# Gather row tables tied to block 124 of U, activation blocks written in halves and full rows, sort constants loaded first

## The chip, the cores and the metric

One core of a Trainium2 chip runs the whole program. The metric is the device time of one execution in microseconds (us); several executions are taken and their median is compared. The core has five engines that run their own instruction queues in order: TensorE (PE) for matmuls, VectorE (DVE), ScalarE (ACT) and GpSimd (POOL) for elementwise work, and SyncE (SP), which here issues nearly all plain DMAs. POOL also issues the indirect DMAs (gathers).

## The reference, cut to what matters

The program is a two-layer decoder trunk for 256 tokens of width 1024. Each layer has a mixer (three attention-like branches) and then the expert stage, which is the part that the change touches:

```python
def peer_ffn(z, wq, subkeys, u_tab, v_tab):        # z: 256 tokens x 1024
    ...
    expert = i1 * PEER_NKEYS + i2                  # 8 heads x 16 picks of 16384 experts, per token
    gate = jax.nn.softmax(score, axis=-1)
    h = jnp.einsum('thkd,td->thk', u_tab[expert], zb)
    act = gate * jax.nn.gelu(h, approximate=False)
    return jnp.einsum('thk,thkd->td', act, v_tab[expert])
```

The tables `u_tab` and `v_tab` have 16384 rows of 1024 float32 numbers per layer.

## The kernel before, in words

The kernel does not gather rows of `u_tab`. It multiplies all 16384 rows with the 256 tokens, in 128 blocks of 128 experts. This is called U. For block `b`, `expert_h` loads 512 KB (`raw<-ut`, by SP, three `raw` buffers), ACT and DVE split it into a high and a low float32r part (`hi`, `lo`, in `split`, line 307), and PE does 24 matmuls of 256 columns (lines 311 to 313). The result goes through Gelu into the activation block `b`: 128 experts on the partitions, 256 tokens as columns. Blocks 0 to 47 lie in the tile `HA`, blocks 48 to 127 in `HB` (SPLIT = 48).

Beside U runs a generator, `gate_map`, which builds the gate factors, four tokens at a time, and multiplies them into all 128 blocks; `self.tok` counts the tokens done. When it has done all 256 tokens, the generator goes on into `lists`, which sorts experts: of blocks 0 to 107 (NC = 108) each partition keeps a list that puts experts used by the first 128 tokens alone first, then those used by both halves, then those used by the second half alone. The sort (fourteen rounds of MAX8 and MATCH_REPLACE8 on DVE) ends in two small tables, `rows` and `vrows`: which row of the activations, and which row of `v`, is next on each partition. It reads constants `quad` and `low`, and keeps its last intermediate, `own`, in a buffer of the tag `oh` (two buffers).

While U runs, the activation blocks 0 to 107 are also written to a DRAM buffer `dA` (shown as `act` in the trace), because the gather reads from there. The function `keep(h, done)` writes them, by SP: four blocks at a time (CHUNK = 4), the half `h` of the tokens in each, so that a row in DRAM is written as two pieces of 512 bytes. Half 0 may be written when 128 tokens are done, half 1 when 256 are. `keep` is called once per block and per half.

After U comes V (`experts_out`): out = activations times `v`. Blocks 108 to 127 are done whole, with plain loads of `v` (`raw<-v`); the first four of them come first. Blocks 0 to 107 are replaced by sorted lists: of the 108 list positions only 98 are done (`FROM1`, `TO0`, `TO1`), and 41 of these for one half of the tokens only. Each position takes two indirect DMAs on POOL, 512 KB of `v` (`HA<-v,vrows`) and 128 KB of activations (`HA<-act,rows`), both into room in the old `HA` tile: seven buffers for `v`, ten for the activations, six positions fetched ahead (FETCH = 6). The gather of activations needs all writes of `dA` to have landed. ACT and DVE then split both (`third` or `hi`/`lo`, and `ah`/`al`), and PE does 12 matmuls of 512 columns for a position with both halves, six for one with one half. Halfway through V stands an `If` on a flag that the sort set; its body is for lists that do not fit, and is skipped here. U and V together take more than half of a layer's time.

The order of instructions on each engine is made by a planner of the framework when the program is built: it moves an instruction forward if its own estimate says that it could run. `self.order(a, b)` tells it that `b` comes after `a` on their engine.

Of the kernel before, what the change touches and what calls it, by code (L numbers as in the profile page):

```python
# [7 lines left out]
F32 = mybir.dt.float32  # L8
# [3 lines left out]
I32 = mybir.dt.int32  # L12
U32 = mybir.dt.uint32
AF = mybir.ActivationFunctionType
OP = mybir.AluOpType
# [3 lines left out]
P = 128  # L19
T = 256  # L20
# [3 lines left out]
NB = 128  # L24
# [7 lines left out]
SPLIT = 48  # L32
# [11 lines left out]
NC = NB - ND  # L44
FROM1, TO0, TO1 = 18, 75, 98
IF_AT, FETCH = 45, 6
CHUNK = 4
ORDER = "rsrrrsrrcsrcrrrnrccrcsrcrrscrncsrrrgnrrrnaagSaSaSSagSgSaggSnggggSagSSnSaagaaaSgSgmSSSamamaSSaagSggSgggggSSmgmmgmmmmmmmmmmmmmmmmmm"
PACE_R, PACE_G = 1.5, 2.25

# [168 lines left out]
class Kernel:  # L219
# [851 lines left out]
    def peer(self, l):  # L1071
        nc, I = self.nc, self.I
        act, dve, pe = nc.scalar, nc.vector, nc.tensor
        with ExitStack() as ctx:
            hp = ctx.enter_context(self.tc.tile_pool(name=f"peer{l}", bufs=1))
            HA = hp.tile([P, SPLIT, T], F32, name="HA")
            sl = hp.tile([P, T // 4, 2, 4], F16, name="sl")
            gp = hp.tile([P, T // 4, 2, 4], F16, name="gp")
            with self.tc.tile_pool(name=f"route{l}", bufs=1) as rp:
                self.z = self.norm_t(self.pvt[:, PV_LN2:PV_LN2 + 8])  # L1080
                if l + 1 < self.layers:
                    self.pvt = self.cp.tile([P, PV_END], F32, tag="pvt", name="pvt")
                    nc.sync.dma_start(self.pvt, I["pv"][l + 1])
                sub = rp.tile([P, 16, P], F32, name="sub")
                nc.sync.dma_start(sub, I["subk"][l])
                qT = rp.tile([P, 16, T], F32, name="qTp")
                self.qdone = 0
                self.deep, self.turn = True, 2
                run = Pace(self.route(rp, sub, qT, (sl, gp)), PACE_R)
                for j in range(16):  # L1090
                    act.copy(qT[:, j], self.proj(I["wq"][l, j], self.z, "sc" if j < 2 else "mm"))
                    self.qdone = j + 1
                    run(1)
                for b in range(SPLIT):
                    self.expert_h(l, b, HA[:, b], None)
                    run(1)
                run(None)
            hp = ctx.enter_context(self.tc.tile_pool(name=f"late{l}", bufs=1))
            HB = hp.tile([P, NB - SPLIT, T], F32, name="HB")
            blk = lambda b: HA[:, b] if b < SPLIT else HB[:, b - SPLIT]  # L1100
            dA = self.dram.tile([NC * P, T], F32, name=f"act{l}")
            self.l, self.hdone, self.tok = l, 0, 0
            kept = [0, 0]

            def keep(h, done):
                b = kept[h]
                n = min(CHUNK, (SPLIT if b < SPLIT else NC) - b)
                if b < NC and self.tok >= P * (h + 1) and b + n <= min(SPLIT + done, NC):
                    src = HA[:, b:b + n] if b < SPLIT else HB[:, b - SPLIT:b - SPLIT + n]
                    hs = slice(h * P, (h + 1) * P)  # L1110
                    nc.sync.dma_start(dA[b * P:(b + n) * P, hs].rearrange("(b p) t -> p b t", p=P), src[:, :, hs])
                    kept[h] += n

            run = Pace(self.gate_map(hp, (sl, gp), HA, HB), PACE_G)
            for b in range(SPLIT, NB):
                self.expert_h(l, b, blk(b), hp, self.tok)
                self.hdone += 1
                run(1)
                keep(0, self.hdone - 1)
                keep(1, self.hdone - 1)  # L1120
            run(None)
            for h in range(2):
                while kept[h] < NC:
                    keep(h, self.hdone)

            if l + 1 < self.layers:
                tiles = [hp.tile([P, D], F32R, tag="oh", name="ready", bufs=2) for _ in range(2)]
                self.ready([I["wa"][l + 1, 0]], tiles)
            if l + 1 == self.layers:
                lnf = hp.tile([P, D], F32, tag="oh", name="lnf", bufs=2)  # L1130
                src = I["lnf"]
                nc.sync.dma_start(lnf, bass.AP(tensor=src.tensor, offset=src.offset, ap=[[0, P], [1, D]]))
                act.mul(lnf, lnf, D ** 0.5)
            self.xnew = self.experts_out(l, hp, HA, blk, dA, l + 1 < self.layers)
            for t in range(2):
                if l + 1 < self.layers:
                    nc.sync.dma_start(self.xd[1][t], self.xnew[t])
            if l + 1 == self.layers:
                self.final(self.xnew, lnf)
# [114 lines left out]
    def expert_h(self, l, b, dst, pool, tok=0):  # L1254
        p = self.proj(self.I["ut"][l, b], self.z)
        if tok < T:
            self.nc.scalar.activation(dst[:, tok:], p[:, tok:], AF.Gelu)
        if tok:
            tmp = pool.tile([P, T], F32, tag="gel", name="gel", bufs=2)
            self.nc.scalar.activation(tmp[:, :tok], p[:, :tok], AF.Gelu)  # L1260
            (self.nc.gpsimd if tok < T else self.nc.vector).tensor_tensor(dst[:, :tok], dst[:, :tok], tmp[:, :tok],  # L1261
                                                                          op=OP.mult)

    def route(self, rp, sub, qT, slots):
        nc, cst = self.nc, self.cst
# [107 lines left out]
    def gate_map(self, hp, slots, HA, HB):  # L1373
        nc = self.nc
        act, dve, pe = nc.scalar, nc.vector, nc.tensor
        sl, gp = slots
        iota2 = hp.tile([P, P, 2], F16, name="iota2")
        oh = hp.tile([P, 4, P, 4], F16, tag="oh", name="iota", bufs=2)
        iota = oh.bitcast(F32).rearrange("p a b c -> p (a b c)")[:, :P]
# [2 lines left out]
        cnt = self.pt([P, 2, P], "tp")  # L1382
        for t0 in range(0, T, 4):
            ts = slice(t0, t0 + 4)
# [24 lines left out]
                act.activation(hb[:, n:], pv[:, SPLIT + n:], AF.Copy, scale=1 / GS)  # L1409
            self.tok = t0 + 4  # L1410
            yield 1.8
        yield from self.lists(hp, cnt)

    def lists(self, hp, cnt):
        nc = self.nc
        act, dve, pe = nc.scalar, nc.vector, nc.tensor
        quad = hp.tile([P, 7, P], F32, name="quad")
        nc.sync.dma_start(quad, self.I["quad"])
        low = hp.tile([P, NC], I32, name="low")
        nc.sync.dma_start(low, self.I["low"])  # L1420
        four = lambda n: hp.tile([P, 2, 4, P], F32, tag="oh", name=n, bufs=2)
        ms, cf = four("ms"), four("cf")
        s = ms[:, 1].rearrange("p a b -> p (a b)")[:, :4 * NC].rearrange("p (a b) -> p a b", a=4)
# [51 lines left out]
        n = -(-NC // 8)  # L1475
# [7 lines left out]
        dve.tensor_scalar(own, ri, P - 1, 7, op0=OP.bitwise_and, op1=OP.logical_shift_left)  # L1483
        dve.tensor_scalar(ri, ri, 3 * P, 2, op0=OP.bitwise_and, op1=OP.logical_shift_right)
        dve.tensor_tensor(own, own, ri, op=OP.bitwise_or)
        self.rows = hp.tile([P, NC], I32, name="rows")
        self.vrows = hp.tile([P, NC], I32, name="vrows")
        dve.tensor_tensor(self.rows, own, low, op=OP.bitwise_or)
        dve.tensor_single_scalar(self.vrows, self.rows, self.l * NB * P, op=OP.bitwise_or)  # L1489
        yield 1.0  # L1490

    def final(self, x, lnf):
        nc = self.nc
# [25 lines left out]
```

## Time and profile before

| | us |
|---|---|
| median of 3 executions (2301.1, 2311.25, 2317.24) | 2311.25 |
| the profiled execution, own time | 2301.95 |
| its span, from first to last instruction | 2300.2 |

The profile is one execution. Times in it count from the start of the span. Layer 0's U blocks after 48 and its V lie between 533 and 1141 us, layer 1's between 1672 and 2286. "Busy" leaves out register, branch and DMA-issuing instructions; matmul ends are modelled, so a count of matmuls per microsecond tells more of PE than its busy share. The granted clock (PEclk) is a share of TensorE's full speed. Where a row ends in brackets, the first number is the time for which the engine had been idle before, and behind the arrow stands what ended it.

### The profile page before, as it was taken

How to read it: one execution, taken by the hardware profiler on the slowest of the kernel's cores; microseconds unless marked ns; L12 is line 12 of the kernel's file. 1: busy time of each engine (PE TensorE's matmuls, PEld its weight loads, DVE VectorE, ACT ScalarE, POOL GpSimd, SP SyncE). 2: the span in 40 equal slices, each digit the busy share in tenths (PEclk: the TensorE clock that was granted, in tenths of full speed). 3: DMA queues.
4: the chain of work that ended last, by engine and by line, in shares of the span. 5: the costliest groups of instructions: out<-in, count | busy, mean ns of one | idle time of the engine just before them, and what ended most of it. 6: DMA issues, size and time to landing. Idle time of an engine off the chain costs nothing. (4 is left out here: it accounts for less than half of the span.)

```text
span 2300.2 us, 43942 instructions
## 1 busy us (share of the span) xinstructions
PE 2236.1 (97%) x16662; PEld 2011.9 (87%) x16662; DVE 1701.4 (74%) x3699; ACT 1146.9 (50%) x2207; POOL 585.4 (25%) x601
## 2 busy tenths in 40 slices
PE   8999999999999999999999999999999999999898
PEld 8888888999999898877798888899999998987686
DVE  6578656996889876766666785769958898666566
ACT  5454434454544345655555444445544443455564
POOL 0001021000112135767600010300001220377674
PEclk9999989999999999999999999999999999999999
DMA  5644226556466887878655432455564758878785
GB/s 188 203 130 120 87 75 217 160 173 196 147 187 188 258 270 254 271 247 259 224 172 190 143 107 70 123 198 167 169 195 142 214 166 274 279 249 267 246 263 164
DMA packets 190152, 439.95 MB, mean 191 GB/s; under 512 B 30134, under 2 KB 90984, under 8 KB 189672
## 3 DMA queue, kind: packets, MB, share of 16 engines
q1 hardware_dynamic: 152008, 308.01, 42.4%
q0 software_dynamic: 37632, 128.48, 17.4%
q8 instruction: 135, 2.21, 0.4%
q14 instruction: 89, 0.73, 0.1%
q10 hardware_dynamic: 288, 0.52, 0.1%
HBM read 403.62 MB, written 33.32 MB: 190 GB/s over the span
## 5 line engine op out<-in xcount | busy, mean ns | idle before, releaser
L311 PE MATMUL mm<-zh,hi 128*128 128x256 f32 x3056 | 891.2, 292 | 9.9 <-ACT hi L307 7.1
L313 PE MATMUL mm<-zh,lo 128*128 128x256 f32 x3056 | 875.3, 287 | 7.4 <-DVE lo L307 7.4
L312 PE MATMUL mm<-zl,hi 128*128 128x256 f32 x3056 | 871.2, 285 | 0.0
L307 DVE TENSOR_TENSOR lo<-raw,hi 128x1024 fp32r<-128x1024 f32 (+1 forms) x468 | 590.5, 1263 | 204.3 <-ACT hi L307 202.6
L307 ACT CAST hi<-raw 128x1024 fp32r<-128x1024 f32 (+1 forms) x468 | 488.5, 1046 | 482.2 <-PE mm L312 310.3
L311 PEld LDWEIGHTS mm<-zh,hi 128*128 128x128 f32 x3056 | 588.3, 193 | 28.5 <-ACT hi L307 9.6
L313 PEld LDWEIGHTS mm<-zh,lo 128*128 128x128 f32 x3056 | 588.1, 192 | 18.9 <-DVE lo L307 10.0
L312 PEld LDWEIGHTS mm<-zl,hi 128*128 128x128 f32 x3056 | 588.7, 193 | 3.8 <-issue 2.9
L271 POOL DMA_INDIRECT HA<-act,rows x196 | 216.8, 1106 | 189.5 <-DVE vrows L1489 59.6
L271 POOL DMA_INDIRECT HA<-v,vrows x196 | 212.7, 1085 | 109.0 <-DVE third L307 38.1
L307 DVE TENSOR_TENSOR lo<-HA,hi 128x1024 fp32r<-128x1024 f32 x132 | 161.6, 1224 | 51.2 <-ACT hi L307 48.7
L1261 POOL TENSOR_TENSOR HB<-HB,gel 128x8 f32<-128x8 f32 (+24 forms) x100 | 82.0, 820 | 385.0 <-ACT gel L1260 336.1
L307 ACT CAST hi<-HA 128x1024 fp32r<-128x1024 f32 x132 | 138.5, 1049 | 30.2 <-PE po L313 25.9
L307 ACT CAST ah<-HA 128x256 fp32r<-128x256 f32 x196 | 79.3, 405 | 117.4 <-PE po L312 115.2
L307 DVE TENSOR_TENSOR al<-HA,ah 128x256 fp32r<-128x256 f32 x196 | 82.9, 423 | 67.5 <-ACT ah L307 24.4
L1409 ACT ACTIVATE HB<-sc 128x300 f32<-128x300 f32 (+38 forms) x128 | 44.8, 352 | 156.2 <-DVE HB L1407 153.2
L307 DVE TENSOR_TENSOR third<-HA,third 128x1024 fp32r<-128x1024 f32 x64 | 78.3, 1223 | 48.7 <-ACT third L307 48.0
L311 PE MATMUL sc<-hi,ah 128*128 128x512 f32 x280 | 94.3, 400 | 16.4 <-ACT hi L307 10.6
L312 PE MATMUL sc<-lo,ah 128*128 128x512 f32 x280 | 100.4, 402 | 1.1 <-DVE lo L307 1.1
L307 ACT CAST third<-HA 128x1024 fp32r<-128x1024 f32 x64 | 67.3, 1051 | 59.4 <-DMA HA<-v,vrows 35.9
L313 PE MATMUL sc<-hi,al 128*128 128x512 f32 x280 | 96.1, 401 | 0.0
L1389 DVE TENSOR_TENSOR oh<-iota,sl 128x1024 f16<-128x1024 f16 x128 | 87.4, 684 | 9.5 <-POOL iota L1381 4.8
(479 smaller groups left out, 3818.8 us busy)
## 6 DMA issues: line engine op xcount, KB each, us to landing
raw<-ut SPq DMA_DIRECT2D x256, 512.0 KB, 3.8
raw<-wa SPq DMA_DIRECT2D x102, 512.0 KB, 3.5
raw<-v SPq DMA_DIRECT2D x40, 512.0 KB, 4.6
raw<-wq SPq DMA_DIRECT2D x32, 512.0 KB, 3.9
act<-HB SPq DMA_DIRECT2D x60, 256.0 KB, 5.2
raw<-wbr SPq DMA_DIRECT2D x24, 512.0 KB, 3.6
act<-HA SPq DMA_DIRECT2D x48, 256.0 KB, 5.1
raw<-cw SPq DMA_DIRECT2D x16, 512.0 KB, 4.4
```

The source lines that it names most:

```text
L271: self.nc.gpsimd.indirect_dma_start(out=dst, out_offset=None, in_=src, in_offset=bass.IndirectOffsetOnAxis(ap=row, axis=0))
L307: return self.nc.scalar.copy(hi, src), self.nc.vector.tensor_tensor(lo, src, hi.bitcast(F32), op=OP.subtract)
L311: return [mm(p, lhsT=l[0], rhs=r[0], start=first, stop=False), mm(p, lhsT=l[0], rhs=r[1], start=False, stop=False), mm(p, lhsT=l[1], rhs=r ...
L312: mm(p, lhsT=l[0], rhs=r[1], start=False, stop=False),
L313: mm(p, lhsT=l[1], rhs=r[0], start=False, stop=last)]
L1261: (self.nc.gpsimd if tok < T else self.nc.vector).tensor_tensor(dst[:, :tok], dst[:, :tok], tmp[:, :tok], op=OP.mult)
L1389: dve.tensor_tensor(oh.rearrange("p n a i j -> p (n a) i j"), iota2[:, None].to_broadcast(full), two(sl), op=OP.is_equal)
L1409: act.activation(hb[:, n:], pv[:, SPLIT + n:], AF.Copy, scale=1 / GS)
```

## The change

- The two instructions that make `rows` and `vrows` move out of `lists` into a function `tables`, which is called after the loop over U; its first instruction is ordered behind the DVE instruction that finishes block 124 (NB - START).
- `keep` writes blocks of `HB` three at a time, not four. Half 0 is written only as long as the gate map has not done all 256 tokens. After that, blocks whose half 0 is in DRAM get their half 1 as before; the others are written once, both halves, in rows of 1024 bytes.
- The loads of `quad` and `low` are issued ahead of `gate_map`'s own constant (`iota`), not at the start of `lists`.

```diff
-CHUNK = 4
+CHUNK, START = (4, 3), 4
...
             def keep(h, done):
                 b = kept[h]
-                n = min(CHUNK, (SPLIT if b < SPLIT else NC) - b)
-                if b < NC and self.tok >= P * (h + 1) and b + n <= min(SPLIT + done, NC):
-                    src = HA[:, b:b + n] if b < SPLIT else HB[:, b - SPLIT:b - SPLIT + n]
-                    hs = slice(h * P, (h + 1) * P)
-                    nc.sync.dma_start(dA[b * P:(b + n) * P, hs].rearrange("(b p) t -> p b t", p=P), src[:, :, hs])
-                    kept[h] += n
+                m = min(CHUNK[b >= SPLIT], (SPLIT if b < SPLIT else NC) - b)
+                if h and b < kept[0]:
+                    m = min(m, kept[0] - b)
+                if b < NC and self.tok >= P * (h + 1) and b + m <= min(SPLIT + done, NC) and (h or self.tok < T):
+                    src = HA[:, b:b + m] if b < SPLIT else HB[:, b - SPLIT:b - SPLIT + m]
+                    ts = slice(h * P if b < kept[0] else 0, h * P + P)
+                    nc.sync.dma_start(dA[b * P:(b + m) * P, ts].rearrange("(b p) t -> p b t", p=P), src[:, :, ts])
+                    kept[h] += m
...
             for b in range(SPLIT, NB):
-                self.expert_h(l, b, blk(b), hp, self.tok)
+                ins = self.expert_h(l, b, blk(b), hp, self.tok)
+                if b == NB - START:
+                    late = ins
                 self.hdone += 1
                 run(1)
                 keep(0, self.hdone - 1)
                 keep(1, self.hdone - 1)
             run(None)
-            for h in range(2):
-                while kept[h] < NC:
-                    keep(h, self.hdone)
+            while kept[1] < NC:
+                keep(1, self.hdone)
+            self.order(late, self.tables(hp))
...
     def gate_map(self, hp, slots, HA, HB):
...
+        quad = hp.tile([P, 7, P], F32, name="quad")
+        nc.sync.dma_start(quad, self.I["quad"])
+        low = hp.tile([P, NC], I32, name="low")
+        nc.sync.dma_start(low, self.I["low"])
+        self.low = low
...
     def lists(self, hp, cnt, quad):
...
-        quad = hp.tile([P, 7, P], F32, name="quad")
-        nc.sync.dma_start(quad, self.I["quad"])
-        low = hp.tile([P, NC], I32, name="low")
-        nc.sync.dma_start(low, self.I["low"])
...
         dve.tensor_tensor(own, own, ri, op=OP.bitwise_or)
+        self.own = own
+
+    def tables(self, hp):
+        dve = self.nc.vector
         self.rows = hp.tile([P, NC], I32, name="rows")
         self.vrows = hp.tile([P, NC], I32, name="vrows")
-        dve.tensor_tensor(self.rows, own, low, op=OP.bitwise_or)
+        first = dve.tensor_tensor(self.rows, self.own, self.low, op=OP.bitwise_or)
         dve.tensor_single_scalar(self.vrows, self.rows, self.l * NB * P, op=OP.bitwise_or)
-        yield 1.0
+        return first
```

`expert_h` now returns its last instruction, the multiplication of the block by its Gelu (line 1261).

## Rows read from the trace of the kernel before

**Rows 1.** The page's first lines: the span, and the busy time of each engine with its share and instructions.

```profile
span 2300.2 us, 43942 instructions
PE 2236.1 (97%) x16662; PEld 2011.9 (87%) x16662; DVE 1701.4 (74%) x3699; ACT 1146.9 (50%) x2207; POOL 585.4 (25%) x601
```

**Rows 2.** Busy time by stretch of layer 0 (start:end, length, then for PE, PEld, DVE, ACT and POOL the busy time and the number of instructions, then granted clock, DMA share, GB/s).

```profile
533.00:545.00 12.00, 12.00 (x108) 11.91 (x107) 7.42 (x9) 5.82 (x11) 0.50 (x2) 1.00 0.74 244
...
785.00:805.00 20.00, 15.38 (x109) 14.34 (x108) 15.25 (x35) 6.32 (x10) 0.00 (x0) 0.91 1.08 344
805.00:831.00 26.00, 25.63 (x191) 25.64 (x192) 24.07 (x48) 12.01 (x18) 0.00 (x0) 0.87 0.66 204
831.00:845.00 14.00, 14.00 (x119) 14.00 (x119) 7.98 (x12) 6.66 (x10) 10.81 (x10) 1.00 0.86 270
845.00:858.00 13.00, 13.00 (x111) 13.00 (x110) 5.95 (x9) 5.40 (x9) 8.72 (x8) 1.00 1.02 402
```

**Rows 3.** The same view of layer 1, the stretch in which its half-1 writes run.

```profile
1923.00:1943.00 20.00, 14.65 (x113) 13.55 (x111) 16.04 (x37) 6.32 (x10) 0.00 (x0) 0.96 1.10 345
```

**Rows 4.** The instructions of line 1111 (the writes of `keep`) on SP's queue, in layer 0 from 640 to 769 us: count, issue time in ns (min/median/max), first and last start.

```profile
L1111 SPq DMA_DIRECT2D act<-HA x12: 377/805/2575, 671.6 to 681.6; - x12
L1111 SPq DMA_DIRECT2D act<-HB x12: 377/455/1382, 684.3 to 760.2; - x12
```

**Rows 5.** The same, from 769 to 831 us.

```profile
L1111 SPq DMA_DIRECT2D act<-HB x18: 450/714/1747, 778.7 to 803.2; - x18
L1111 SPq DMA_DIRECT2D act<-HA x12: 377/606/1252, 769.5 to 781.8; - x12
```

**Rows 6.** The DMA view of 769 to 805 us: packets by size, and the main queue's packets, MB and share of the time of 16 engines.

```profile
DMA packets 15986, 11.55 MB, mean 321 GB/s; under 512 B 568, under 2 KB 14975, under 8 KB 15982
...
q1 hardware_dynamic: 15982, 11.50, 104.4%
```

**Rows 7.** The main queue in the DMA view of 545 to 580 us, where nearly all traffic is loads in rows of 4 KB.

```profile
q1 hardware_dynamic: 1693, 6.15, 56.3%
```

**Rows 8.** DVE in order of time, layer 0 (start, duration, line, operation): the multiplications that finish blocks 99, 109 and 124 (line 1261), and the instruction that makes `vrows`.

```profile
775.15 0.42 DVE L1261 TENSOR_TENSOR HB<-HB,gel 128x256 f32<-128x256 f32 x1
...
816.02 0.42 DVE L1261 TENSOR_TENSOR HB<-HB,gel 128x256 f32<-128x256 f32 x1
...
831.18 0.22 DVE L1489 TENSOR_SCALAR vrows<-rows 128x108 int32<-128x108 int32 x1
...
857.49 0.42 DVE L1261 TENSOR_TENSOR HB<-HB,gel 128x256 f32<-128x256 f32 x1 [0.72 <-ACT gel L1260]
```

**Rows 9.** DVE in order of time, layer 1: the end of MAX8's last round, `vrows`, and block 124.

```profile
1964.96 0.60 DVE L1478 MAX8 ms<-cf 128x8 f32<-128x432 f32 x1
...
1968.81 0.22 DVE L1489 TENSOR_SCALAR vrows<-rows 128x108 int32<-128x108 int32 x1
...
1994.61 0.42 DVE L1261 TENSOR_TENSOR HB<-HB,gel 128x256 f32<-128x256 f32 x1 [0.72 <-ACT gel L1260]
```

**Rows 10.** SP's queue in order of time, layer 1: the load of the last norm's weights, which takes over a buffer of the tag `oh`.

```profile
1965.64 0.33 SPq L1132 DMA_DIRECT2D lnf<-lnf  x1
```

**Rows 11.** POOL in order of time, layer 0: gathers number 1, 6 (the first of `v`), 17 and 18, the gather of `v` for the tenth and the 37th position, and the first gather of `v` behind the `If`.

```profile
831.45 1.18 POOL L271 DMA_INDIRECT HA<-act,rows  x1 [59.60 <-DVE vrows L1489]
...
838.59 1.32 POOL L271 DMA_INDIRECT HA<-v,vrows  x1 [0.30 <-issue]
...
854.89 0.96 POOL L271 DMA_INDIRECT HA<-act,rows  x1 [0.30 <-issue]
870.32 2.01 POOL L271 DMA_INDIRECT HA<-v,vrows  x1 [14.47 <-DVE third L307]
...
882.35 0.94 POOL L271 DMA_INDIRECT HA<-v,vrows  x1 [0.81 <-DVE lo L307]
...
957.18 1.25 POOL L271 DMA_INDIRECT HA<-v,vrows  x1 [0.30 <-issue]
...
996.34 0.94 POOL L271 DMA_INDIRECT HA<-v,vrows  x1 [8.78 <-DVE third L307]
```

**Rows 12.** Time to landing of the gathers of `v` (both layers, 196 of them).

```profile
DMA to landing us min/median/max: 4.2/5.0/11.0
```

**Rows 13.** ACT in order of time at the start of V, layer 0: the second whole block's load is split; then the first gathered rows of `v` (`third`), then both operands of the third whole block; and the activations of the fourth. Below them the splits of the `v` rows of the tenth and the 37th position.

```profile
866.28 1.05 ACT L307 CAST hi<-raw 128x1024 fp32r<-128x1024 f32 x1 [2.07 <-DMA raw<-v]
...
867.51 1.04 ACT L307 CAST third<-HA 128x1024 fp32r<-128x1024 f32 x1
868.44 0.41 ACT L307 CAST ah<-HB 128x256 fp32r<-128x256 f32 x1
868.75 1.06 ACT L307 CAST hi<-raw 128x1024 fp32r<-128x1024 f32 x1
871.07 0.41 ACT L307 CAST ah<-HB 128x256 fp32r<-128x256 f32 x1 [1.26 <-PE po L312]
...
897.90 1.05 ACT L307 CAST hi<-HA 128x1024 fp32r<-128x1024 f32 x1 [0.53 <-PE po L313]
...
967.90 1.05 ACT L307 CAST hi<-HA 128x1024 fp32r<-128x1024 f32 x1
```

**Rows 14.** PE in order of time: the first matmuls of the third whole block of V.

```profile
871.11 0.63 PE L311 MATMUL sc<-hi,ah 128*128 128x512 f32 x2
```

**Rows 15.** The loads of the gate map's and the sort's constants on SP's queue, both layers (count, issue time in ns, first and last start).

```profile
L1380 SPq DMA_DIRECT2D iota<-iota x2: 327/327/327, 533.2 to 1672.2; - x2
L1418 SPq DMA_DIRECT2D quad<-quad x2: 424/425/426, 533.6 to 1672.6; - x2
```

More of the change, by code (lines that the diff above doesn't have):

```diff
@@ L1260, in expert_h @@
             self.nc.scalar.activation(tmp[:, :tok], p[:, :tok], AF.Gelu)
-            (self.nc.gpsimd if tok < T else self.nc.vector).tensor_tensor(dst[:, :tok], dst[:, :tok], tmp[:, :tok],
-                                                                          op=OP.mult)
+            return (self.nc.gpsimd if tok < T else self.nc.vector).tensor_tensor(dst[:, :tok], dst[:, :tok], tmp[:, :tok],
+                                                                                 op=OP.mult)
     def route(self, rp, sub, qT, slots):
@@ L1411, in gate_map, with lists @@
             yield 1.8
-        yield from self.lists(hp, cnt)
-    def lists(self, hp, cnt):
+        yield from self.lists(hp, cnt, quad)
+    def lists(self, hp, cnt, quad):
         nc = self.nc
         act, dve, pe = nc.scalar, nc.vector, nc.tensor
-        quad = hp.tile([P, 7, P], F32, name="quad")
-        nc.sync.dma_start(quad, self.I["quad"])
-        low = hp.tile([P, NC], I32, name="low")
-        nc.sync.dma_start(low, self.I["low"])
         four = lambda n: hp.tile([P, 2, 4, P], F32, tag="oh", name=n, bufs=2)
```

## The prediction

> **What bounds the kernel now.** I read the page's first lines, then busy time by stretch around the end of U, then SP, DVE, POOL and ACT in order of time there. PE is busy for 97% of the span and DVE for 74% [rows 1], so only a stretch in which PE falls below its rate can give time back. PE's full rate in U is read where nothing holds it: 119 matmuls in 14 us and 111 in 13 us, 8.5 per us at a granted clock of 1.00 [rows 2]; a block of 24 matmuls then takes 2.82 us.
>
> Three places matter to this change. First the burst of writes after the gate map has ended: 30 chunks of 256 KB between 769 and 803 us in layer 0 [rows 5]. From 785 to 831 us PE does 109 + 191 = 300 matmuls where 46 x 8.5 = 391 fit, so 91 are missing: 10.7 us, part of it through the clock, which was granted at 0.91 and 0.87 there after PE had run dry [rows 2]. Block 109 is finished 40.9 us after block 99, where ten blocks take 28.2 us: 12.6 us by that reading [rows 8]. Layer 1 loses 57 of 170 matmuls, 6.7 us, in 20 us of the same stretch [rows 3]. So the burst costs some 10 us per layer. Second the end of U, from 831 to 858 us: 17 gathers are issued there and the DMA engines move up to 402 GB/s, yet PE keeps its full rate [rows 2, 11]. Third V, where POOL issues a gather every 1.3 to 1.6 us without rest from 882 us on, some 10 to 15 us ahead of the splits that need them [rows 11, 13].
>
> **The table held back.** `vrows` is made at 831.18 us in layer 0 and 1968.81 in layer 1; block 124 ends at 857.49 + 0.42 and 1994.61 + 0.42 [rows 8, 9]. With `rows` and `vrows` behind it, the first gather moves from 831.45 to about 858.5 us, 27 us later, and in layer 1 by 26 us. DVE does the same two instructions, under 0.5 us together. On U this brings nothing, since PE is full in the stretch that the gathers leave.
>
> What is late next is the first `v` row set. It is the sixth gather, 838.59 - 831.45 = 7.1 us behind the first [rows 11]: 858.5 + 7.1 = 865.6, and with the median landing of 5.0 us [rows 12] it is there at 870.6. Today ACT splits it at 867.51, in front of the operands of the third whole block (868.44 and 868.75), in one in-order queue [rows 13]. If ACT's order stays, that split ends at 870.6 + 1.04 = 871.6, the block's `ah` at 872.0, its `hi` at 873.0 and `lo`, on DVE 1.2 us behind, at 874.3; PE's first four matmuls on `hi` take 0.9 us of this. PE wants the block at 871.11 [rows 14]. Stall: 1.9 + 0.4 = 2.3 us per layer. Bounds: nothing, if the planner puts the gathered split behind the whole block's, since the first four whole blocks need no gather; with a landing of 11.0 us [rows 12], 8.3 us. I take 2.3, as the median landing is the nearest row.
>
> Behind it in POOL's queue stand all other gathers. The first 17 take 854.89 + 0.96 - 831.45 = 24.4 us, so the 18th goes at 882.9 where it went at 870.32 (it had waited 14.5 us for its buffer). By the tenth position's `v`, four gathers on, POOL is at 888.9 where it was at 882.35: 6.6 us late, since the idle time before it has been used up [rows 11]. That lag stays, as POOL has no rest until the `If`. Positions had a lead (gather to split) of 897.90 - 882.35 = 15.5 us, and 967.90 - 957.18 = 10.7 us at the tightest place [rows 11, 13]. Less 6.6, and with V itself 2.3 later, 11.2 and 6.4 us are left, more than the 5.0 us of a landing. I take nothing; the bound is 11.0 - 6.4 = 4.6 us per layer. At the `If` POOL waits for the other engines, 8.8 us [rows 11]: a lag of 6.6 us ends there, and the second half of V is as before.
>
> `own` keeps its `oh` buffer 27 us longer. In layer 1 the norm weights' load, with U loads behind it on SP, takes over such a buffer; it goes at 1965.64, when MAX8 has just let go of the other one, and before `rows` [rows 9, 10]. It doesn't wait for `own`: nothing.
>
> **The writes.** `keep` runs once per block. Before, 24 chunks leave ahead of the end of the gate map, 12 of `HA` and 12 of `HB` [rows 4]. The gate map does 2.25 / 1.8 = 1.25 steps of four tokens per block, so 128 tokens are done after 25 blocks of `HB`, all after 51; 26 calls for half 0 lie between (blocks 25 to 50), 12 go to `HA` and 14 to `HB`, now three blocks each: 42, so that 18 blocks (90 to 107) are left for full rows. The burst becomes 12 chunks of 256 KB, 14 of 192 and six of 384: 32 issues in place of 30, and 8,064 in place of 7,680 KB, as 14 chunks of 192 KB went ahead and not 12 of 256. Rows of 512 bytes fall from 15,360 to 11,520, and 2,304 rows of 1 KB come.
>
> The price of a row: loads of 4 KB took 0.563 x 35 us x 16 / 1693 = 186 ns each [rows 7]. The burst's 15,982 packets took 1.044 x 36 x 16 = 601 us; less 1,007 loads at 186 ns, 414 us remain for 14,975 short ones: 27.7 ns [rows 6]. What a row of 1 KB costs is not in the trace: 46.5 ns as a quarter of a 4 KB row, 55.4 as two short ones. The 3,840 short rows saved are worth 106 us of engine time, the new rows cost 107 to 128: on 16 engines the burst grows by 0 to 1.3 us. Two SP issues more (0.6 to 0.7 us each [rows 5]) lie beside transfers. I take 0.5 us per layer, nearer the 4 KB price, and hold that the burst stays as harmful as it is: it still starts all at once, when the gate map ends.
>
> The Trainium skill (Advanced Engine Details and Errata, Clock Domains) gives 42 to 43 ns for an unobstructed row of 1 KB. By that the burst would shrink by 0.5 us per layer and the sum be 2 us less; no run here shows such a row, and the trace's 512-byte row at 27.7 ns is no unobstructed one.
>
> **The constants.** `quad` is issued at 533.6 us already, 0.4 us behind `iota`: the planner had moved it up [rows 15]. Now it is ahead of `iota`, and the gate map may start some 2 us later, the landing of 448 KB. DVE is busy for only 7.4 of 12 us there and PE is full [rows 2]; the sort's end no longer sets the gathers' start. I take nothing; without that cover it is 2 us per layer.
>
> **Sum.** Two layers of 2.3 + 0 + 0.5 + 0 = 2.8 us: 5.6 us on 2301.95, 2307.6 us. The profiled execution is 9.3 us under the median of 2311.25, and the executions differ by 16 us among themselves, so I set the median at half that offset: 2307.6 + 4.7 = 2312 us.
>
> **The rivals.** (a) The burst is eased: full rows and fewer short packets let the U loads through. For it: the loss sits exactly where these writes run. Against it: more bytes, one more chunk kind, the same start. It decides where a 1 KB row costs clearly under 46 ns (106 us / 2,304), or where the new order on SP lets a load pass earlier. From here on the base is 2301.95 + 4.7 = 2306.6. Half the loss returned is 10 us in all: 2306.6 - 10 = 2297; all of it, 21 us: 2286.
> (b) The gathers' absence helps U's tail. The one wait for a load there is 2.1 us before the split at 866.28 [rows 13]; taken away in both layers and with no stall in V, -4 us: 2302. The Trainium skill (DMA: Bandwidth & Descriptors, Issuing engines are not separate DMA queues) states that transfers of all issuers share the same 16 engines; the trace agrees (402 GB/s with both), but PE shows no loss by it.
> (c) POOL becomes V's bound: the head start of 24 us was needed. Landings grow as six row sets of 512 KB now meet the whole blocks' loads, PE waits 4 to 8 us at the start of V and 2 to 4.6 before the `If`: 8 per layer gives 2306.6 + 16 = 2323, the ends of both terms with the writes at 1.3 us (8.3 + 4.6 + 1.3 = 14.2 per layer) 2335. It decides where a landing takes over 6.4 us. For it: the leads shrink all the way to the `If`.
> (d) Nothing shows: the planner reorders the splits, and everything else is hidden: 2307.
>
> **Chances.** Forecast 0.42, (c) 0.25, (b) and (d) together 0.20, (a) 0.13. About 1% is what a measurement of this kernel tells from no change: under 2288 or over 2334. Only the full version of (a) goes below: 0.04. Of (c) the upper part goes above: 0.10. Within 1%: 0.86. The range takes in the half version of (a) and most of (c), and the spread of the executions: 2297 to 2331, with 1 in 10 left out at either end. The forecast's own range, with the V stall at 0 to 5 and the write term at 0 to 1.3 per layer, is 2307 to 2319.
>
> **What would show it.** In the profile after: the first gather at 858 us or later; about 32 writes between the gate map's end and block 107, with 300 matmuls or fewer in the 46 us that are 785 to 831 now; `third` at the start of V ending ACT's wait on a gather of `v`; leads 4 to 7 us shorter up to the `If`, the same behind it; POOL's wait at the `If` shorter than 8.8 us. Wrong, if PE's matmuls in the burst rise by 30 or more (rival a), or if waits on `HA<-v,vrows` put gaps into PE before the `If` (rival c), or if POOL still starts before block 124.

## The result, and the profile after

| | before | after |
|---|---|---|
| median of six executions each, same chip (us) | 2307.98 | 2321.85 |
| lowest to highest (us) | 2301.1 to 2317.24 | 2320.29 to 2325.76 |
| ratio after / before, 95% interval | | 1.0051 [1.003, 1.0072] |
| the profiled execution, own time (us) | 2301.95 | 2325.76 |

The change costs half a per cent: 0.0051 x 2308 = 11.8 us by the ratio, 13.9 by the medians. The forecast was 2312, inside a range of 2297 to 2331. The two profiled executions lie 23.8 us apart, since that of before is among its fastest and that of after the slowest of its six; some 10 us between the two profiles can't be put down to the change. So stretches are compared below, not ends.

Busy time by stretch, layer 0 of the kernel after, in the columns of [rows 2]:

```profile
785.00:805.00 20.00, 15.91 (x129) 15.16 (x127) 15.91 (x39) 6.38 (x11) 0.00 (x0) 1.00 1.08 342
805.00:831.00 26.00, 24.79 (x183) 24.58 (x184) 22.77 (x42) 12.05 (x19) 0.00 (x0) 0.87 0.69 211
831.00:845.00 14.00, 14.00 (x119) 14.00 (x118) 7.41 (x11) 6.55 (x10) 0.00 (x0) 1.00 0.60 178
845.00:858.00 13.00, 13.00 (x111) 13.00 (x110) 6.78 (x9) 6.35 (x10) 0.00 (x0) 1.00 0.60 193
```

PE does 129 + 183 = 312 matmuls in the 46 us of the burst; before it did 300 [rows 2]. U's end is full in both, 119 and 111. POOL is now idle there, and the DMA engines move 178 to 193 GB/s where they moved up to 402.

The writes, in layer 1 of the kernel after (count, issue time in ns, first and last start), first ahead of the end of the gate map, then behind it:

```profile
L1113 SPq DMA_DIRECT2D act<-HB x14: 360/434/2561, 1834.8 to 1888.9; - x14
...
L1113 SPq DMA_DIRECT2D act<-HA x12: 377/683/1711, 1823.1 to 1833.2; - x12
```
```profile
L1113 SPq DMA_DIRECT2D act<-HB x20: 386/620/1332, 1932.5 to 1955.1; - x20
...
L1113 SPq DMA_DIRECT2D act<-HA x12: 378/613/1290, 1920.8 to 1931.9; - x12
```

That is 32 issues in the burst, 20 of them of `HB`. The DMA view of 769 to 805 us answers to [rows 6]:

```profile
DMA packets 15002, 11.77 MB, mean 327 GB/s; under 512 B 616, under 2 KB 14056, under 8 KB 14998
...
q1 hardware_dynamic: 14998, 11.73, 106.4%
```

What a full row of 1 KB takes is read where nearly nothing else moves, from 1949.4 to 1953.4 us, in layer 1:

```profile
DMA packets 1528, 1.55 MB, mean 387 GB/s; under 512 B 62, under 2 KB 1513, under 8 KB 1528
...
q1 hardware_dynamic: 1528, 1.55, 110.7%
```

The start of V is where the profiles part. DVE (the table), POOL (the first, third, tenth and eleventh gathers) and ACT, all in layer 0 of the kernel after, in order of time:

```profile
858.78 0.27 DVE L1497 TENSOR_TENSOR rows<-ms,low 128x108 int32<-128x108 int32 x1
859.09 1.22 DVE L307 TENSOR_TENSOR ready<-raw,ready 128x1024 fp32r<-128x1024 f32 x1
860.23 0.21 DVE L1498 TENSOR_SCALAR vrows<-rows 128x108 int32<-128x108 int32 x1
```
```profile
859.35 2.01 POOL L271 DMA_INDIRECT HA<-act,rows  x1 [88.93 <-DVE rows L1497]
...
863.04 0.95 POOL L271 DMA_INDIRECT HA<-act,rows  x1 [0.30 <-issue]
...
873.13 0.95 POOL L271 DMA_INDIRECT HA<-act,rows  x1 [0.30 <-issue]
874.38 0.94 POOL L271 DMA_INDIRECT HA<-v,vrows  x1 [0.30 <-issue]
```
```profile
872.19 0.41 ACT L307 CAST ah<-HA 128x256 fp32r<-128x256 f32 x1 [1.45 <-PE po L312]
879.68 1.04 ACT L307 CAST hi<-HA 128x1024 fp32r<-128x1024 f32 x1 [7.09 <-DMA HA<-v,vrows]
880.64 0.40 ACT L307 CAST ah<-HB 128x256 fp32r<-128x256 f32 x1
880.95 1.04 ACT L307 CAST hi<-raw 128x1024 fp32r<-128x1024 f32 x1
```

Ten gathers of activations now go ahead of the first `v`, where five did [rows 11]: it leaves 15.0 us after the first gather, not 7.1. ACT, in order, waits 7.09 us for its rows (874.38 to 879.68), with the next whole block's operands (880.64, 880.95) behind it. PE, in order of time, layer 0 and layer 1, stops for what ACT splits behind its wait:

```profile
874.79 0.40 PE L313 MATMUL po<-hi,al 128*128 128x512 f32 x1
880.78 1.22 PE L311 MATMUL sc<-hi,ah 128*128 128x512 f32 x2 [5.59 <-ACT hi L307]
...
2033.51 0.73 PE L311 MATMUL sc<-hi,ah 128*128 128x512 f32 x2 [3.90 <-ACT hi L307]
```

In layer 1 the order of the gathers is the old one, five and then `v`, and ACT waits at another split, `third`. `fetch` gives the buffer `third` to each third position (`n % 3 == 2`), so this split needs the third gather of `v`, the eighth in all. The first gather of `v`, issued at 2019.77 us, landed after 4.1 us; the third, issued at 2022.69, after 8.4. POOL, layer 1, then the view of the third gather alone (who waited for it, for how many us and how often, and its landing), then ACT:

```profile
2012.81 1.08 POOL L271 DMA_INDIRECT HA<-act,rows  x1 [89.64 <-DVE vrows L1498]
...
2019.77 0.94 POOL L271 DMA_INDIRECT HA<-v,vrows  x1 [0.30 <-issue]
...
2022.69 1.75 POOL L271 DMA_INDIRECT HA<-v,vrows  x1 [0.30 <-issue]
```
```profile
L271 POOL DMA_INDIRECT HA<-v,vrows x1: 1752/1752/1752, 2022.7 to 2022.7; - x1
...
  ACT third L307: 6.0, 1
...
DMA to landing us min/median/max: 8.4/8.4/8.4
```
```profile
2031.16 1.04 ACT L307 CAST third<-HA 128x1024 fp32r<-128x1024 f32 x1 [6.00 <-DMA HA<-v,vrows]
```

To compare all kernels I cut U's end and V's start by four marks: the start of DVE's multiplications that finish blocks 99, 109 and 127, and the start of the split of the seventh gathered row set of `v`. Microseconds between them, layer 0 / layer 1:

| | 99 to 109 (burst) | 109 to 127 (U's end) | 127 to seventh `v` (V's start) |
|---|---|---|---|
| before | 40.9 / 39.8 | 52.5 / 51.8 | 19.6 / 20.3 |
| after | 40.7 / 41.0 | 52.7 / 54.0 | 26.9 / 25.4 |

V's start is longer by 7.2 and 5.1 us, 12.4 together, the size of the measured loss. From there to the `If` 98.2 us pass in layer 0 in both (888.11 to 986.29, and 893.92 to 992.11), and 98.5 and 98.8 in layer 1. From the seventh split to the last one V takes 255.2 and 256.3 us before, 257.4 and 258.6 after.

### The profile page after: what moved, and what is told of

Same layout as the page of the kernel before. It is cut to its first block, busy times and chain, and to the rows that moved or that the text cites. A ratio compares the mean times of both kernels' runs of the same rounds, so it can differ in the third digit from the quotient of the medians.

```text
span 2324.0 us, 43975 instructions
## 1 busy us (share of the span) xinstructions
PE 2245.5 (97%) x16662; PEld 2017.0 (87%) x16662; DVE 1702.2 (73%) x3699; ACT 1145.4 (49%) x2207; POOL 584.6 (25%) x601
## 5 line engine op out<-in xcount | busy, mean ns | idle before, releaser
L271 POOL DMA_INDIRECT HA<-v,vrows x196 | 210.5, 1074 | 80.2 <-DVE al L307 36.8
L307 ACT CAST hi<-HA 128x1024 fp32r<-128x1024 f32 x132 | 138.6, 1050 | 38.8 <-PE po L313 26.9
L307 ACT CAST ah<-HA 128x256 fp32r<-128x256 f32 x196 | 79.3, 405 | 119.1 <-PE po L312 114.1
L307 ACT CAST third<-HA 128x1024 fp32r<-128x1024 f32 x64 | 67.3, 1051 | 68.8 <-DMA HA<-v,vrows 42.6
```

What stands on the lines that cost most here:

```text
L271: self.nc.gpsimd.indirect_dma_start(out=dst, out_offset=None, in_=src, in_offset=bass.IndirectOffsetOnAxis(ap=row, axis=0))
L307: return self.nc.scalar.copy(hi, src), self.nc.vector.tensor_tensor(lo, src, hi.bitcast(F32), op=OP.subtract)
```

## The experiments

They ran in three groups, each on a chip of its own. The kernel before takes 2378.1, 2358.5 and 2360.5 us there, 2 to 3% more than in the first result; I call the chip of the first result the first chip, and take it for a fourth, though its number is not on record. Landing times are not shown in the traces of the groups. Each ratio is against the kernel before on the chip of its own group.

### The parts alone (first group)

The table held back, with old writes and old constants (the load of `low` and `quad` stays in `lists`):

```diff
+                ins = self.expert_h(l, b, blk(b), hp, self.tok)
+                if b == NB - 4:
+                    late = ins
...
+            self.order(late, self.tables(hp))
```

> The kernel before with one part of the change: rows and vrows made behind block 124; writes and constants as before. Theory G (the first rows of v come late to the start of V, because the held table puts ten gathers of activations ahead of them on POOL): 1.004 to 1.006 of the kernel before, PE waiting 4 to 6 us for the split of the first v rows at the start of each V. Theory W (the writes in three-block chunks and full rows make the burst longer): 0.999 to 1.001. Theory C (the constants put ahead of iota delay the gate map): 0.999 to 1.001.

The new writes alone, with the old table:

```diff
-CHUNK = 4
+CHUNK = (4, 3)
...
-            for h in range(2):
-                while kept[h] < NC:
-                    keep(h, self.hdone)
+            while kept[1] < NC:
+                keep(1, self.hdone)
```
(and the new `keep`)

> The kernel before with the new keep alone (three-block chunks, full rows for late blocks). Theory G: 0.999 to 1.002, no wait of PE at the start of V; the burst's matmul loss within 2 us per layer of that before. Theory W: 1.004 to 1.006, with the loss in the burst 4 to 6 us per layer larger. Theory C: 0.999 to 1.001.

The kernel after with the first gathers on POOL put in pairs, `v` first:

```diff
+            pair = [self.gather(I["v"], ...), self.gather(dA, ...)]
+            if not rest and n < 10:
+                chain.extend(pair[n >= 7:])
+                self.order(*chain[-2 - (7 > n > 0):])
```

> The changed kernel with POOL's first gathers ordered in pairs, v ahead of activations for each position, so that the first v rows are asked for as POOL's first gather and not its eleventh. Theory G: the wait of 4 to 6 us at the start of V is gone, 1.000 to 1.002 of the kernel before. Theory L (the total of POOL's late start is what counts, whatever comes first): the same 17 gathers start at the same time, so PE waits as long before the If, 1.004 to 1.006. Theories W and C: 1.004 to 1.006, unchanged.

The kernel after with the table tied to block 116 instead of 124:

```diff
-CHUNK, START = (4, 3), 4
+CHUNK, START = (4, 3), 12
```

> The changed kernel with START = 12: the table is made behind block 116, eight blocks (23 us) sooner. Theory G and theory L: POOL starts 23 us sooner, the waits at the start of V go, 0.999 to 1.002 of the kernel before. Theories W and C: 1.004 to 1.006, since writes and constants are as in the changed kernel.

| | ratio [95%] | burst | U's end | V's start |
|---|---|---|---|---|
| table held alone | 0.9989 [0.9969, 1.0008] | 39.8 / 40.6 | 52.2 / 52.2 | 31.3 / 27.3 |
| writes alone | 0.9981 [0.9955, 1.0008] | 42.7 / 41.8 | 63.8 / 60.8 | 19.7 / 20.3 |
| after, `v` first | 1.002 [0.9998, 1.0042] | 41.4 / 40.7 | 52.1 / 52.7 | 21.7 / 28.7 |
| after, block 116 | 0.9964 [0.9942, 0.9986] | 42.3 / 41.4 | 54.6 / 53.1 | 26.1 / 22.3 |

Theory G alone (the held table only costs, at V's start) falls here: V's start is 7 to 12 us longer per layer than with the early table, as it should be, and yet the table held alone costs nothing in the whole. The other side is in U's end. Busy time by stretch, first of the kernel with the writes alone (gathers beside U), then of the table held alone:

```profile
831.00:845.00 14.00, 14.00 (x117) 13.83 (x115) 6.24 (x8) 4.83 (x8) 11.14 (x10) 1.00 0.87 288
845.00:858.00 13.00, 6.61 (x29) 5.82 (x29) 2.77 (x4) 3.62 (x6) 6.82 (x7) 0.61 0.83 314
```
```profile
831.00:845.00 14.00, 14.00 (x119) 14.00 (x118) 7.40 (x11) 6.54 (x10) 0.00 (x0) 1.00 0.63 183
845.00:858.00 13.00, 13.00 (x111) 13.00 (x109) 6.11 (x8) 5.88 (x9) 0.00 (x0) 1.00 0.61 192
```

With gathers beside it PE does 29 matmuls in 13 us, and the granted clock is 0.61; without them 111 at 1.00. What PE lacks is a load of U: ACT, in order of time, with the writes alone:

```profile
846.65 0.38 ACT L1261 ACTIVATE gel<-mm 128x256 f32<-128x256 f32 x1
855.71 1.04 ACT L307 CAST hi<-raw 128x1024 fp32r<-128x1024 f32 x1 [8.68 <-remote]
```

("remote" stands for a releaser that this trace does not resolve; the instruction needs only `raw`, so I read it as the landing of the load.) What the DMA engines did in that wait shows in busy time from 847 to 855 us, and in the two queues of the DMA view: q0, which carries POOL's gathers, and q1, the plain transfers of SP. First the kernel with the writes alone, then the kernel before on the first chip, which has issued about as many gathers by then:

```profile
847.00:855.00 8.00, 5.67 (x24) 4.91 (x24) 1.34 (x2) 0.03 (x1) 5.31 (x6) 0.56 1.02 399
...
q0 software_dynamic: 725, 2.53, 79.3%
q1 hardware_dynamic: 194, 0.67, 23.0%
```
```profile
847.00:855.00 8.00, 8.00 (x69) 8.00 (x68) 3.59 (x6) 2.63 (x5) 6.26 (x6) 1.00 1.02 411
...
q0 software_dynamic: 604, 2.16, 67.5%
q1 hardware_dynamic: 313, 1.13, 34.7%
```

The engines are full in both. Where PE starves, the gathers hold 79% of them and U's loads get 0.67 MB; where it doesn't, the loads get 1.13 MB. (The share of 0.83 above is lower because hardly anything moved from 855 to 858 us, where the share was 0.19.) On this chip the early gathers make U's loads late, which [rows 2] didn't show for the first chip. I called the theory of both sides T.

Theory W (the writes lengthen the burst) gets 0.9981, no loss.

### Two repeats, the kernel before against itself, and both remedies together (second group)

The kernel after again, the kernel before again, the table held alone again, and `v` first with block 116 (both edits above):

> The changed kernel once more, beside the kernel before, so that its time stands beside the other runs of this call. Theory G (late first v rows at the start of V, nothing gained in U's tail): 1.004 to 1.006. Theory T (two-sided: where gathers in U's tail make the U loads late, the held table gives back some 10 us per layer there, and takes about as much at the start of V): 1.003 to 1.007 if the kernel before runs at about 2308 us, 0.997 to 1.002 if it runs at about 2378 us as in the runs before this one.

> The kernel before itself, for its trace beside the others of this call. Theory T: if it runs at about 2378 us, PE loses 8 us or more between the end of the gate map's writes and block 124, where 17 gathers run beside the U loads, as it does in the kernel with the new writes alone; at about 2308 us it loses nothing there. Theory G: nothing lost there in either.

> The kernel before with the held table alone, once more. Theory T: within 0.2% of the changed kernel of this call (writes and constants do nothing). Theory W (the writes cost or give something): the changed kernel differs from it by 0.3% or more.

> The changed kernel with the table behind block 116 and POOL's first gathers in pairs, v first. Theory T: neither loss is there in full: 0.994 to 0.999 on a run like the slow ones, 0.999 to 1.002 on one like the first. Theory G: 0.999 to 1.001 on both.

| | ratio [95%] | burst | U's end | V's start |
|---|---|---|---|---|
| after | 1.0033 [1.0014, 1.0053] | 40.7 / 41.6 | 52.1 / 53.9 | 31.6 / 27.1 |
| before against itself | 1.0025 [1.0001, 1.005] | 39.8 / 39.0 | 54.8 / 64.8 | 19.7 / 20.3 |
| table held alone | 1.0024 [1.0003, 1.0045] | 41.2 / 42.6 | 52.7 / 52.2 | 26.9 / 27.2 |
| after, `v` first, block 116 | 1.0005 [0.9981, 1.0028] | 40.1 / 39.4 | 49.7 / 51.0 | 25.1 / 22.3 |

The kernel before against itself reads 1.0025: on these chips a difference under about 0.3% can't be told from none, and the 1.0024 and 1.0033 say hardly more than that. Its trace repeats the finding on U's end, now in the kernel before itself. Busy time by stretch, layer 1:

```profile
1980.00:2000.00 20.00, 18.77 (x153) 18.36 (x152) 11.49 (x22) 7.49 (x11) 9.52 (x10) 1.00 0.77 253
2000.00:2016.00 16.00, 9.18 (x38) 8.12 (x38) 4.49 (x6) 4.08 (x6) 7.84 (x8) 0.60 0.78 289
2016.00:2032.00 16.00, 16.00 (x132) 16.00 (x132) 7.05 (x10) 6.60 (x10) 0.00 (x0) 0.98 0.51 155
```

38 matmuls in 16 us while POOL issues eight gathers, 132 as soon as it issues none. From 2000 to 2008 us the gathers' queue held 93.5% of the DMA engines and the loads' 6.9%, with the old writes, so the new writes are not what starves PE. T had put this loss at 8 us or more at a time of about 2378 us; at 2366 layer 1 lost 13 against the first chip (64.8 for 51.8), layer 0 only 2 (54.8 for 52.5).

### Where the price of a late table shows clearly (third group)

The table tied to block 127 (START = 1); `v` first with START = 8; the kernel before with `v` first; the kernel after a third time:

```diff
-CHUNK, START = (4, 3), 4
+CHUNK, START = (4, 3), 1
```

> The changed kernel with START = 1: the table behind block 127, three blocks (8.5 us) later still. Theory T (the price is the wait for the first v rows at the start of V; U's tail has no more to give): the first six positions come 7 to 10 us later in each layer than in the changed kernel, so 14 to 20 us in all, 1.006 to 1.009 of it, and the stretch from block 109 to block 127 stays at 52 to 54 us. Theory L (POOL's lag, absorbed by leads of 10 us and more and ended at the If): within 0.2% of the changed kernel.

> The changed kernel with the table behind block 120 and POOL's first gathers in pairs, v first: the first v rows are asked for some 27 us sooner before they are needed than in the changed kernel (11.4 us by the table, 14 us by the order). Theory T: the start of V as in the kernel before (block 127 to the seventh position in 20 to 23 us, not 26 to 31), U's tail at 50 to 53 us; 0.994 to 0.997 of the changed kernel of this call, and 0.997 to 1.001 of the kernel before. Theory W or C: as the changed kernel.

> The kernel before with POOL's first gathers in pairs, v first; table, writes and constants as before. Theory T: the first rows are there long before V needs them in either order, so nothing changes at the start of V; 0.998 to 1.002. If the order on POOL by itself were worth something, 0.995 to 0.998.

> The changed kernel once more beside these three. Theory T: 1.003 to 1.006 of the kernel before on a run like the first, 0.998 to 1.004 on a slower one; block 127 to the seventh position takes 25 us or more in both layers.

| | ratio [95%] | burst | U's end | V's start |
|---|---|---|---|---|
| after, block 127 | 1.0113 [1.0082, 1.0145] | 40.8 / 38.6 | 52.7 / 54.4 | 39.5 / 36.3 |
| after, `v` first, block 120 | 1.0009 [0.9976, 1.0041] | 42.3 / 41.2 | 51.8 / 59.9 | 25.2 / 19.6 |
| before, `v` first | 0.9991 [0.9966, 1.0015] | 41.7 / 40.0 | 63.2 / 54.0 | 19.8 / 20.3 |
| after | 1.0019 [1.0, 1.0038] | 40.1 / 40.4 | 52.0 / 52.8 | 29.3 / 25.3 |

Three blocks later is the one clear difference: 1.0113. POOL (the first gather, and the eleventh, the first of `v`), ACT and PE at V's start, in order of time, of the kernel after with block 127:

```profile
868.18 2.22 POOL L271 DMA_INDIRECT HA<-act,rows  x1 [97.71 <-DVE rows L1497]
...
882.69 0.94 POOL L271 DMA_INDIRECT HA<-v,vrows  x1 [0.31 <-issue]
```
```profile
887.08 1.04 ACT L307 CAST hi<-HA 128x1024 fp32r<-128x1024 f32 x1 [10.97 <-DMA HA<-v,vrows]
```
```profile
888.17 1.22 PE L311 MATMUL sc<-hi,ah 128*128 128x512 f32 x2 [12.28 <-ACT hi L307]
```

It is the picture of the kernel after with the gathers 8.2 us later (they start at 860.02 us there, on the same chip); PE's stop grows from 5.6 to 12.3 us. Against the kernel after of its group the time is 2385.35 / 2363.91 = 1.009, the upper end of T's 1.006 to 1.009.

Taken together, on the three slower chips (each figure the mean of one profiled execution's two layers per kernel): with the early table (writes alone, before again, before with `v` first) U's end takes 60.2 us and V's start 20.0; with the table at block 124 and the planner's order of gathers (held alone twice, after twice) 52.5 and 28.2. Holding it back saves 7.7 us per layer and costs 8.2. That is +1.0 us for both layers; the four ratios are 0.9989, 1.0024, 1.0033 and 1.0019, with a mean of 1.0016, or 3.9 us, in the noise of 0.25% beside it. From the seventh split of `v` to the last one they take the same, 278.1 us per layer with the early table and 279.2 with the late one. At block 127 the sum of both stretches is 92.2 and 90.7 against 80.2: +22.5 us, and 0.0113 x 2360 = 26.7 was measured (the profiled execution, at 2372.49, is the fastest of its six, so the two needn't meet closely). So T holds for when the table is made, by the stretches and by the one ratio that stands out; its forecasts for the remedies do not, as the next paragraph says.

The remedies are not settled. The order of POOL decides V's start in layer 0: 21.7 us with `v` first at block 124 (table of the first group), against 26.9 to 31.6 in the four without. In layer 1, where only five gathers of activations go ahead anyway, the wait at `third` went from 5.6 to 6.5 us to 0.3, but V's start got no shorter (28.7 against 25.3 to 27.3): other waits took its place, some of which the trace doesn't resolve. Block 116 shortens V's start to 22.3 in layer 1. T's forecast for block 120 with `v` first failed: 0.994 to 0.997 of the kernel after of its group, where 2366.27 / 2363.91 = 1.001 came. There the gathers meet U's loads again. U's end takes 59.9 us in layer 1, and from 2036 to 2044 us PE does 27 matmuls, with 73.5% of the DMA engines for the gathers' queue and 21.1% for the loads'. For block 116 with `v` first T had 0.994 to 0.999, and 1.0005 came. 0.9964, 1.0005, 1.0009 for the versions with an earlier table don't agree, and the remainder of V differs by some 10 us from one profile to the next. No version beats the kernel before by more than the noise on two chips.

## Why the prediction came out as it did

The forecast was right in its range and its direction, and not in size: 5.6 us were added for the change, 11.8 to 13.9 came. The parts were not run alone on the first chip; what is said of it rests on the stretches of its two profiles.

**The step that was mis-sized** is the one at V's start: "What is late next is the first `v` row set. It is the sixth gather, 838.59 - 831.45 = 7.1 us behind the first". The kind of loss was right: a wait on `HA<-v,vrows` in ACT's queue, with the third whole block's operands behind it, and a gap in PE. The term was put at 2.3 us per layer; V's start grew by 7.2 and 5.1. Two inputs were wrong before any run:

- The split at 867.51 [rows 13] is of `third`, so it is not of the first row set of `v` but of the third. That is the eighth gather, issued at 841.47 us, 10.0 us behind the first.
- The landing was the median of all 196 gathers, 5.0 us. The first seven of `v`, the ones in question, took longer already then. Their landing in layer 0, before:

```profile
DMA to landing us min/median/max: 6.6/8.5/9.9
```

In layer 1 both show. ACT waited for the third row set, which left 9.9 us behind the first gather and took 8.4 us to land: 18.3 us, where the prediction had 12.1. With 10.0 in place of 7.1 and the landing left at 5.0, its own sum gives 5.2 us. In layer 0 the orders on POOL and ACT changed as well. ACT took the first row set first, and that was now the eleventh gather, 15.0 us behind the first, with a landing of 5.2 us. The order of the gathers had been read off the old trace, where the table was ready long before. Ten gathers of activations go ahead where another DVE instruction stands between `rows` and `vrows` (here `ready`, so that `vrows` starts 1.45 us behind `rows`). So it is in layer 0 of all five profiles with the table at block 124 and the planner's order on POOL; at block 127 ten and eight go ahead, with such an instruction in both layers; and wherever none stands between, in that order, five do. That the planner orders them so because of this split fits every layer, but is argued: no run moved only that split. That the order is what costs in layer 0 is shown by the run with `v` first (V's start 21.7 instead of 26.9 to 31.6).

PE also ran slower after the stop of 5.59 us: the granted clock was 0.50 from 880.7 to 884.3 us, the lower of its two levels, with eight matmuls in 3.6 us, and 1.00 behind it, with 17 in 3.7. This was not in the sum either; it is in the 7.2.

**POOL's lag, taken as nothing**, held up to the `If`. From the seventh `v` to there 98.2 us pass in both kernels. The lead of the 37th position, which the prediction took for the tightest place, shrank to 7.7 us from 10.7 in layer 0 (6.4 expected); in layer 1 it had been 7.5 and is 7.7. The mark given for the `If` itself failed: POOL's wait did not get shorter. POOL, in order of time, kernel after, behind the `If`:

```profile
992.31 1.06 POOL L271 DMA_INDIRECT HA<-act,rows  x1 [0.30 <-DVEq L1225]
993.68 1.54 POOL L271 DMA_INDIRECT HA<-v,vrows  x1 [0.30 <-issue]
995.53 0.95 POOL L271 DMA_INDIRECT HA<-act,rows  x1 [0.30 <-issue]
1005.27 0.94 POOL L271 DMA_INDIRECT HA<-v,vrows  x1 [8.79 <-DVE al L307]
```

It is 8.79 us as before [rows 11], only two gathers later; it is a wait for a buffer. The leads of the first two positions behind it are 4.6 and 4.7 us (before 7.0 and 5.0). The next row set that ACT splits, issued at 1015.93 us, took 7.9 us to land and held ACT back for 8.80 us and PE for 6.5; before, the same place had a wait of 4.03 in layer 0 and of 10.48 in layer 1. In all, V behind the seventh split is 2.2 to 2.3 us longer in each layer than before, nearly all of it behind the `If`; with one profile of either kernel on this chip, it is not shown that the lag caused this. In layer 0 V's additions start 8.0 us later than before (1155.54 for 1147.54).

**The writes, 0.5 us per layer.** 32 issues, as counted. Over all profiles ten blocks of the burst take 40.5 us with the old writes (five kernels, ten layers) and 41.0 with the new (nine kernels): +0.4, at the predicted size, in a scatter of 38.6 to 42.7 that would hide it. The price of a full row, which the prediction had between 46.5 and 55.4 ns, can be read. From 1949.4 to 1953.4 us the queue took 1.107 x 4 x 16 = 70.8 us; less 15 loads at some 200 ns and 62 packets of a few bytes, about 67 us are left for 1,451 rows of 1 KB, or 46 ns. Two short ones take 55, so merging saves some 9 ns. The 2,304 new rows then cost 107 us, as much as the 3,840 short ones saved (106), so the term was nearer to nothing than to 0.5. Rival (a) needed clearly under 46 ns and is out. It also wanted 30 more matmuls; there were 12. (The prediction's 186 and 27.7 ns count the packets under 512 bytes of [rows 6] as rows; without them a load takes some 210 ns and a short row 27, which changes none of this.)

**The constants, nothing.** `iota` goes 0.9 us later (534.13 in place of 533.2 [rows 15]), yet block 99 is finished at 773.72 us where it was at 775.15 [rows 8]. The constants alone were not run.

**Rival (b) was under-priced**, and by the wrong row. The text said that U's end is full, so that taking the gathers away brings nothing. On the first chip that is so in both profiles, though even there the loads of U landed after a median of 5.7 us between 831 and 858 us beside the gathers, and 3.6 without them. That the kernel before scatters by 16 us over six executions and the kernel after by 5.5 would fit a U's end that stalls in some executions and not in others; no trace of those shows it. On the other three chips the stall is there in all three kernels profiled with an early table, 54 to 65 us in all six layers where 18 blocks at 2.82 us need 50.8. The Trainium skill (DMA: Bandwidth & Descriptors, Issuing engines are not separate DMA queues) says that transfers of all issuers interleave on the same 16 engines; these traces agree, with both queues together at 102% of the engines from 847 to 855 us on either chip.

**Rival (c)** has the number: 2323 was worked out for it, 2321.85 came. Half of its mechanism is there, 4 to 8 us at V's start, with landings over the 6.4 us that it asked for (8.4 in layer 1); the other half, 2 to 4.6 us before the `If`, is not. That it came out at the measured time is in part luck. The sign that the prediction set for this rival, gaps in PE by waits on `HA<-v,vrows` before the `If`, came with 5.59 and 3.90 us; the forecast's own stall at V's start would have shown the same sign, so it could not tell the two apart. Besides the mark for POOL's wait at the `If`, two others failed: 312 matmuls where 300 or fewer were named, and leads that are 3 us shorter in layer 0 alone, not 4 to 7. The forecast's own range ended at 2319.

Open remains why the other chips take 50 to 70 us more. Where they do shows: with the early table, V behind the seventh split takes 278.1 us per layer where the first chip took 255.2 and 256.3, and U's end 60.2 where it took 52.5 and 51.8, some 61 us for both layers. Why the gathers get more of the DMA engines there is open too, and whether a table tied to block 116 with `v` first is worth anything: 0.9964 and 1.0005 for block 116 allow both.

## What to carry to other kernels

Holding back a table that starts a queue of transfers has two prices, one in the stage that it leaves (contention with that stage's loads) and one in the stage that it feeds (the lost head start); read each from its own stage, and give the first a price even where one profile shows its engine full. When a step is moved next to its users, their order on the queue has to be worked out anew: what was first in the old trace was so because everything had long been ready. Find out which transfer a split really waits for (the name of its buffer told it here), and take a landing time from the transfers in question, not from the median of all. An order set by hand took one wait away here and brought no time in the whole; run the kernel against itself before believing in 0.3%.

## What the hardware showed that was not expected

- The same kernel took 2308, 2358, 2360 and 2378 us (medians) on four chips, the first taken for a fourth; on any one of them its executions spread over 16 to 23 us.
- Gathers beside plain loads left PE at full rate on one chip (111 matmuls in 13 us) and held U's loads back on another (29 matmuls in 13 us, with a wait of 8.68 us on ACT). The DMA engines were full in both, 1.02 from 847 to 855 us; the gathers' queue held 67.5% of them on the first and 79.3% on the second.
- A gather of `v` (512 KB) landed after 5.0 us in the median; the first seven of a layer took 6.0 to 11.0 us in the kernel before, beside U's loads, and 4.1 to 8.8 in the kernel after, beside V's first loads.
- In a full queue of writes to DRAM a row of 1 KB took some 46 ns and one of 512 bytes some 27: half the rows, but only a sixth less time.
